# Weight sums in 64 DRAM transfers, gate weights ahead of the norm vectors, and a fixed plan for the norm between two projections

## The chip, the core and the metric

The kernel runs on one core of a Trainium2 chip. The metric is the device time of one execution in microseconds. The core has five engines, each with a queue of its own: TensorE (PE), VectorE (DVE), ScalarE (ACT), GpSimd (POOL) and SyncE (SP), which only issues transfers. DRAM and the on-chip buffers are joined by 16 DMA engines.

## What is computed

A small encoder with two mixer layers over 1024 tokens of width 1024, all in float32. Cut to what matters:

```python
for i in range(2):
    h = rms_norm(x, norm_g[i])
    y = mixer_a(h, ...) if i == 0 else mixer_b(h, ...)   # attention, 16 heads, ending in "@ w_out"
    x = x + y
    g = sigmoid(rms_norm(x, ple_norm_g[i]) @ ple_w_gate[i])
    x = x + g * (p[i] @ ple_w_proj[i])
return rms_norm(x, final_norm_g)
```

Between the output projection (`@ w_out`) and the gate projection (`@ ple_w_gate`) lies one RMS norm over the whole row of 1024, so a token tile can enter the gate projection only when both its halves have come out of the output projection.

## The kernel before

**Products.** A float32 product is made of three fast products: each operand is split into a high part (`wh`, `HTh`) and a low part (`wl`, `HTl`), and PE adds wh*HTh, wl*HTh and wh*HTl (L317). One [128 x 512] block with a contraction of 512 is 12 matmuls. Tokens are kept in 8 tiles of 128 rows. To enter a product, a normalised tile `xn` is transposed on PE four 128x128 pieces at a time (L445) into `t`, copied by ACT as `HTh` (L446), and DVE makes `HTl` (L447).

**Weights.** A queue object `WQ` brings weights in units of 512 KB. `stage` issues the load of a unit on SP (L209, into `wstage`), at most two units ahead of the split; `pump`, called once a step, splits one staged unit that is at least `age` steps old: ACT makes the high part (L226), DVE the low part one step later (L231). `hold` names a unit that isn't loaded yet.

**Mixer A (layer 0)** runs heads h = 0 to 15 with 8 steps j each. A step takes attention work of one head and fills PE with projection blocks. At j = 1 the bias table of the next head is built by POOL (L676, `tb<-MK,u`). POOL also multiplies the finished outputs by their gate (L531, `Y<-Y,G`) and by the softmax's reciprocal (L532, `Y<-Y,rb`), and SP stores them to DRAM (L524, `yD0h`). ACT's copy of a new output into a Y buffer (L497, `Y<-o`) has to wait for the store that last read that buffer.

**Weight sums.** The output projection is one Strassen level with sums of weight quarters, t1 to t4. `weight_sums` (L581 to L600) makes them in DRAM while mixer A runs, for both layers: 16 jobs of 1 MB, of which 8 are plain copies issued by SP (L589, as 16 rows of 16384) and 8 are accumulating transfers issued by POOL (L592, as 256 rows of 1024). A head from h = 1 on pops one job at j = 2 and one at j = 6 (L912).

**Dense phase.** `dense_phase(l)` (from L1437) follows each mixer. `strassen_out` yields after each of its last eight blocks, n = 0 to 7, in the order (5,0), (5,1), (3,0), (5,2), (3,1), (5,3), (3,2), (3,3); kind 5 completes a right half of tile 4+m, kind 3 that of tile m, each by one DVE addition (`fold`, L1388). Left halves are complete before: those of tiles 4 to 7 in the four "t4" blocks, those of tiles 0 to 3 by `second` (L1342). From n = 8 on the gate projection's first half (hf = 0) runs block by block in the order of tiles 0, 4, 0, 4, 1, 5, 1, 5 and so on. For the norm between them, ACT sums squares of half rows (L1473), DVE makes the reciprocal root of a pair of tiles m and 4+m (L1482 and ten small operations, L328 to L336), DVE scales the two tiles (L1500), and then the transposes follow. What is done at a step is decided by queues: `folded`, `squared`, `ready`, `pend`. At n = 0 two norm vectors are loaded (`load_gain`, L421), and then the gate weights are staged by `pump`; at n = 1 ACT takes the squares of all eight left halves in a row. A finished gate block is combined with `pp` (loaded from DRAM by L1593): L1541 (tanh), L1542, L1543. At the last tile of hf = 0 of layer 0, `rope_tables` has POOL make two tables (L1658) and SP store them with four transfers (L1661); after this the `pp` loads of hf = 1 are issued. In hf = 1 the finished tiles are squared, normed, and transposed for the next mixer (L1642, L445).

Of the kernel before, what the change touches and what calls it, by code (L numbers as in the profile page):

```python
# [11 lines left out]
F32 = mybir.dt.float32  # L12
# [9 lines left out]
NT = 8  # L22
# [136 lines left out]
def trunk(ctx, tc, x, wts, rpb, gains, hgains, mask, rope, gain0, out):  # L159
# [421 lines left out]
    def weight_sums():  # L581
        jobs = []

        def quarter(l, hf, u):
            i = UNIT["out", l, hf, u]
            return wts[i:i + 2]

        def copy(l, n, src):
            jobs.append(lambda: sync.dma_start(tD[l][n].rearrange("u p c -> (u p) c"), src.rearrange("u p c -> (u p) c")))  # L589

        def plus(l, n, src):
            jobs.append(lambda: pool.dma_start(tD[l][n].rearrange("u p c -> (u p) c"),  # L592
                                               src.rearrange("u p c -> (u p) c"), accum_op=ALU.add, max_dma_last_dim=4096))
# [666 lines left out]

    def strassen_out(l, X, ps_d, ps_t):
        xs = x if l == 0 else xD
# [174 lines left out]
    def dense_phase(l):  # L1437
        with ExitStack() as es:
# [20 lines left out]

            def pend_ht():  # L1460
                clock[0] += 1
                if pend and pend[0][0] <= clock[0]:
                    to_ht(ps_t, *pend.pop(0)[1:])

            ready = []
            folded, squared = [], []
            junk = one.tile([128, D], BF16, name="junk")
# [6 lines left out]

            def roots(n):
                if squared and squared[0][0] < n:
                    m = squared.pop(0)[1]
                    sm = slice(2 * m, 2 * m + 2)
                    r = sb.tile([128, 2], F32, name="rn", bufs=4)
                    wk = sb.tile([128, 8], F32, name="wkn", bufs=2)  # L1480
                    half = sa[:, 1, sm]
                    dve.scalar_tensor_tensor(half, half, 0.5 / D, sa[:, 0, sm], op0=ALU.mult, op1=ALU.add)  # L1482
                    rsqrt(r, half, wk)
                    ready.append(((m, 4 + m), r))

            def squares(n):
                while folded and folded[0][0] < n:
                    t = folded.pop(0)[1]
                    square(t, 1)
                    if t < 4:  # L1490
                        squared.append((n, t))

            def scale_pair():
                if not ready or len(pend) > 4:
                    return
                ts, r = ready.pop(0)
                xs = []
                for i, t in enumerate(ts):
                    xn = xalloc()
                    dve.scalar_tensor_tensor(xn, X[t], r[:, i:i + 1], g1, op0=ALU.mult, op1=ALU.mult)  # L1500
                    xs.append(xn)
                pend.extend([(clock[0] + 2, t, xn, (c,)) for c in range(2) for t, xn in zip(ts, xs)])

            for n, (step, m) in enumerate(strassen_out(l, X, ps_d, ps_t)):
                if n == 0:
# [3 lines left out]
                    WQ.cap[4] = 2  # L1509
                    WQ.hold = ("bg", 0) if l == 0 else None  # L1510
                    g1 = load_gain(sb, 2 * l + 1, 2)
                    g2 = load_gain(sb, 2 * l + 2, 2)
                    WQ.age, WQ.lag, age, lag = 2, 0, WQ.age, WQ.lag
                if n == 1:
                    for t in range(NT):
                        square(t, 0)
                if n == 2:
                    dve.tensor_scalar(sa[:, 0], sa[:, 0], 0.5 / D, 0.5 * EPS, op0=ALU.mult, op1=ALU.add)
                folded.append((n, m + 4 if step == 5 else m))
# [5 lines left out]
            WQ.age, WQ.lag = age, lag  # L1525

            for kind in ("ple",):
# [3 lines left out]
                for hf in range(2):  # L1531
# [69 lines left out]
                    for t, i in order:  # L1601
# [3 lines left out]
                        parts[t][i]()  # L1605
                        n += 1
                        WQ.pump()
                        pend_ht()
                        squares(n)
                        roots(n)  # L1610
                        scale_pair()
# [35 lines left out]
    def rope_tables(sb):  # L1647
# [3 lines left out]
        rt = sb.tile([128, 1024], F32, name="xn", bufs=4)  # L1651
        sync.dma_start(rt.rearrange("p (i t d) -> p i t d", i=2, t=NT), rope)
        for kind in range(2):
            ro = sb.tile([128, 1024], F32, name="xn", bufs=4)
            for i in range(2):
# [3 lines left out]
                                   rt[:, s].rearrange("p (t d) -> p t d", t=NT), gb, ALU.mult)  # L1659
            for i in range(2):  # L1660
                sync.dma_start(ropeD[kind, :, :, i].rearrange("t p d -> p t d"),  # L1661
                               ro[:, i * 512:(i + 1) * 512].rearrange("p (t d) -> p t d", t=NT))

# [24 lines left out]
```

## Time and profile before

| | |
|---|---|
| runs | 1551.56, 1554.64 and 1555.78 us, median 1554.64 us |
| profiled execution | 1561.72 us, of which its span is 1559.9 us |
| mean granted TensorE clock | 0.99 |
| busy time of PE | 1511.1 us (97%) in 8976 matmuls |
| busy time of DVE | 1097.7 us (70%) |
| busy time of ACT | 902.3 us (58%) |
| busy time of POOL | 287.1 us (18%) |
| transfers | 157.21 MB in 89943 packets, mean 101 GB/s |

The profiled execution is one of its own and 7.1 us slower than the median of the three runs. A row of the timeline gives start and duration of an instruction (or of several alike), its line, its operands as out<-in, and in brackets how long the engine was idle before it and what ended that. PEclk is the granted clock as a share of full speed. In these traces q1 is the queue of the transfers that SP issues, q0 that of POOL's.

Where things lie in time: mixer A up to about 545 us, the output projection of layer 0 up to about 622, its gate projection up to about 740, mixer B up to about 1370, then the dense phase of layer 1.

### The profile page before, as it was taken

How to read it: one execution, taken by the hardware profiler on the slowest of the kernel's cores; microseconds unless marked ns; L12 is line 12 of the kernel's file. 1: busy time of each engine (PE TensorE's matmuls, PEld its weight loads, DVE VectorE, ACT ScalarE, POOL GpSimd, SP SyncE). 2: the span in 40 equal slices, each digit the busy share in tenths (PEclk: the TensorE clock that was granted, in tenths of full speed). 3: DMA queues.
4: the chain of work that ended last, by engine and by line, in shares of the span. 5: the costliest groups of instructions: out<-in, count | busy, mean ns of one | idle time of the engine just before them, and what ended most of it. 6: DMA issues, size and time to landing. Idle time of an engine off the chain costs nothing.

```text
span 1559.9 us, 24298 instructions
## 1 busy us (share of the span) xinstructions
PE 1511.1 (97%) x8976; PEld 1319.8 (85%) x8976; DVE 1097.7 (70%) x2113; ACT 902.3 (58%) x1801; POOL 287.1 (18%) x389
## 2 busy tenths in 40 slices
PE   9998999999999999999999999999999999999897
PEld 8887988988988887778988889989999888778686
DVE  7564476477477598747877776777877777687856
ACT  6564465366366635433466767666767777644332
POOL 1311222113112000010132122453131200000022
PEclk9999999999999999999999999999999999999999
DMA  8325256242122862253210111111101112662214
GB/s 260 125 94 132 64 170 179 53 113 92 35 85 70 322 242 95 82 149 124 79 51 15 38 38 49 44 33 42 57 30 46 50 62 96 206 230 91 99 50 139
DMA packets 89943, 157.21 MB, mean 101 GB/s; under 512 B 17376, under 2 KB 53344, under 8 KB 89696
## 3 DMA queue, kind: packets, MB, share of 16 engines
q1 hardware_dynamic: 85056, 139.66, 26.8%
q0 software_dynamic: 2176, 8.39, 2.9%
q10 hardware_dynamic: 2592, 7.61, 1.4%
q8 instruction: 71, 1.16, 0.3%
q14 instruction: 48, 0.39, 0.1%
HBM read 125.10 MB, written 50.83 MB: 113 GB/s over the span
## 4 chain that ended last, share of the span: by engine, by line
PE 40%; DVE 7%; ACT 3%; issue 2%; DMA 0%; SPq 0%; ACTq 0%; DVEq 0%
PE d L317 19%; PE o L317 7%; PE t L1173 6%; PE s L317 6%; DVE PTl L1176 1%; DVE mn L1157 1%; ACT PTh L1175 1%; ACT P L1163 1%; PE t L317 1%; DVE wl L231 1%; PE t L445 0%; DMA wstage<-in_wts 0%; PE t L1127 0%; DVE t L991 0%; ACT wh L226 0%
## 5 line engine op out<-in xcount | busy, mean ns | idle before, releaser
L317 PE MATMUL d<-wh,HTh 128*128 128x256 f32 (+1 forms) x1032 | 348.9, 340 | 13.5 <-ACT th L642 7.7
L317 PE MATMUL d<-wh,HTl 128*128 128x256 f32 (+1 forms) x1032 | 342.1, 333 | 5.1 <-DVE HTl L447 5.1
L317 PE MATMUL d<-wl,HTh 128*128 128x256 f32 (+1 forms) x1032 | 341.1, 332 | 0.0
L1176 DVE TENSOR_TENSOR PTl<-t,PTh 128x512 fp32r<-128x512 f32 x256 | 164.4, 683 | 111.0 <-ACT PTh L1175 110.7
L317 PEld LDWEIGHTS d<-wh,HTh 128*128 128x128 f32 x1032 | 197.2, 192 | 35.2 <-ACT th L642 8.1
L317 PEld LDWEIGHTS d<-wh,HTl 128*128 128x128 f32 x1032 | 197.4, 192 | 25.7 <-DVE HTl L447 6.6
L317 PEld LDWEIGHTS d<-wl,HTh 128*128 128x128 f32 x1032 | 197.6, 192 | 19.1
L317 PE MATMUL d<-HTh,wh 128*128 128x512 f32 x504 | 205.8, 408 | 0.0
L317 PE MATMUL d<-HTh,wl 128*128 128x512 f32 x504 | 198.2, 393 | 0.0
L317 PE MATMUL d<-HTl,wh 128*128 128x512 f32 x504 | 197.5, 392 | 0.0
L1163 ACT ACTIVATE P<-s,mn 128x1024 f32<-128x1024 f32 x128 | 142.8, 1115 | 59.2 <-DVE mn L1157 58.4
L1175 ACT ACTIVATE PTh<-t 128x512 fp32r<-128x512 f32 x256 | 140.2, 593 | 44.6 <-PE t L1173 44.0
L1157 DVE TENSOR_REDUCE mn<-s 128x1 f32<-128x1024 f32 x128 | 154.7, 1209 | 12.2 <-PE s L317 12.2
L1173 PE MATMUL t<-ident,P 128*128 128x128 f32 x1024 | 137.2, 275 | 5.8 <-DVE PTl L1176 4.0
L317 PE MATMUL s<-KA,QS 128*128 128x512 f32 (+2 forms) x384 | 133.5, 402 | 0.0
L1173 PEld LDWEIGHTS t<-ident,P 128*128 128x128 f32 x1024 | 114.7, 140 | 21.0 <-DVE PTl L1176 15.3
L722 DVE TENSOR_TENSOR PTl<-t,PTh 128x384 fp32r<-128x384 f32 (+1 forms) x128 | 66.6, 520 | 85.2 <-ACT PTh L721 84.0
L231 DVE TENSOR_TENSOR wl<-wstage,wh 128x1024 fp32r<-128x1024 f32 x78 | 100.0, 1286 | 37.5 <-ACT wh L226 36.9
L317 PE MATMUL s<-KB,QS 128*128 128x512 f32 (+2 forms) x384 | 121.6, 371 | 0.0
L317 PE MATMUL o<-PTh,V 128*128 128x256 f32 (+2 forms) x672 | 118.9, 288 | 1.2 <-DVE Y L461 0.9
L317 PE MATMUL o<-PTl,V 128*128 128x256 f32 (+2 forms) x672 | 119.1, 288 | 0.1
L317 PEld LDWEIGHTS d<-HTh,wl 128*128 128x128 f32 x504 | 94.6, 188 | 21.7
(237 smaller groups left out, 2681.5 us busy)
## 6 DMA issues: line engine op xcount, KB each, us to landing
wstage<-in_wts SPq DMA_DIRECT2D x88, 512.0 KB
pp<-ppD SPq DMA_DIRECT2D x32, 256.0 KB
X<-in_x SPq DMA_DIRECT2D x15, 512.0 KB
rb<-rD SPq DMA_DIRECT2D x56, 128.0 KB
ppD<-th SPq DMA_DIRECT2D x20, 256.0 KB
xD<-X SPq DMA_DIRECT2D x8, 512.0 KB
X<-xD SPq DMA_DIRECT2D x8, 512.0 KB
out<-xn SPq DMA_DIRECT2D x7, 512.0 KB
```

The lines of the kernel that those rows point to most:

```text
L231: eng.tensor_tensor(lo[:, c:c + n], s[:, c:c + n], hi[:, c:c + n], ALU.subtract)
L317: pe.matmul(ps, a, b, start=first, stop=last, skip_group_check=True)
L722: dve.tensor_tensor(PTl[:, sl], ps[:, :m], PTh[:, sl], ALU.subtract)
L1157: dve.tensor_reduce(mn, ps, axis=AX.X, op=ALU.min)
L1163: act.activation(p, ps, AF.Exp, bias=mn, scale=-1.0, accum_out=RS[h, hf][:, t:t + 1])
L1173: pe.transpose(ps[:, i], p[:, k * 128:(k + 1) * 128], ident)
L1175: act.activation(PTh[:, ks, c], ps, AF.Copy)
L1176: dve.tensor_tensor(PTl[:, ks, c], ps, PTh[:, ks, c], ALU.subtract)
```

## The change

It has four parts.

1. Each copy and each accumulating transfer of the weight sums is cut in four: 64 jobs of 256 KB, copies of 16 rows of 4096 (L593 of the kernel after) and sums of 64 rows of 1024 (L597). One is popped at each step of a head but j = 1, from h = 1 on.
2. At the last `second`, before n = 0, the first two gate-weight units are staged at once, ahead of the loads of the norm vectors; `age` is 1 in place of 2 in these steps and 2 in the gate projection's first half. Units of the second half are held until n = 11.
3. The squares of the left halves are taken one by one, each right after the step that completes the half (`early`), and those of a right half right after its fold. The reciprocal roots, the scalings and the transposes follow a table (`norms`): roots and scaling of pair 0 at n = 3, of pair 1 at n = 5, the roots of pairs 2 and 3 together at n = 8, their scalings at n = 9 and n = 11. Transposes go up to two groups a step.
4. The four stores of the rope tables are issued after the `pp` load that follows tile 0 of hf = 1, in place of before the first `pp` loads of hf = 1.

```diff
         def copy(l, n, src):
-            jobs.append(lambda: sync.dma_start(tD[l][n].rearrange("u p c -> (u p) c"), src.rearrange("u p c -> (u p) c")))
+            for i in range(4):
+                jobs.append(lambda i=i: sync.dma_start(rows(tD[l][n], i, 4), rows(src, i, 4)))
 
         def plus(l, n, src):
-            jobs.append(lambda: pool.dma_start(tD[l][n].rearrange("u p c -> (u p) c"),
-                                               src.rearrange("u p c -> (u p) c"), accum_op=ALU.add, max_dma_last_dim=4096))
+            for i in range(4):
+                jobs.append(lambda i=i: pool.dma_start(rows(tD[l][n], i, 4), rows(src, i, 4),
+                                                       accum_op=ALU.add, max_dma_last_dim=4096))
...
-                        if h >= 1 and j in (2, 6) and jobs:
+                        if h >= 1 and j != 1 and jobs:
                             jobs.pop(0)()
...
             dve.tensor_tensor(xt, xt, P1[m], ALU.add)
+            early(1, m)
...
                 fold(xt0 + m, xc, Y[m], op)
+                if wk == "t4":
+                    early(4, m)
                 pulse()
...
-                pend.extend([(clock[0] + 2, t, xn, (c,)) for c in range(2) for t, xn in zip(ts, xs)])
+                    xs.append((t, xn))
+                pend.extend([(clock[0] + age + c, t, xn, (c,)) for c in range(2) for t, xn in xs])
...
+            norms = {
+                1: [prep],
+                3: [lambda: roots(0, 1), lambda: scale_pair(0)],
+                5: [lambda: roots(1, 1), lambda: scale_pair(1)],
+                8: [lambda: roots(2, 2)],
+                9: [lambda: scale_pair(2)],
+                11: [lambda: scale_pair(3)],
+            }
+
+            def early(kind, m):
+                if kind == 4:
+                    square(4 + m, 0)
+                if kind == 1 and m < 3:
+                    square(m, 0)
+                if kind == 1 and m == 3:
+                    square(3, 0)
+                    WQ.hold = ("ple", l, 1, 0)
+                    WQ.stage(True)
...
-                if n == 1:
-                    for t in range(NT):
-                        square(t, 0)
...
+                square(m + 4 if step == 5 else m, 1)
                 WQ.pump()
-                pend_ht()
-                squares(n)
-                roots(n)
-                scale_pair()
+                for f in norms.get(n, ()):
+                    f()
+                pend_ht(True)
...
                         if l == 0 and hf == 0 and t == seq[-1]:
-                            rope_tables(sb)
+                            rope_stores = rope_tables(sb)
                         load_pp(seq.index(t) + 2)
+                        if l == 0 and hf == 1 and t == 0:
+                            rope_stores()
```

**Mixer A, SP, around the store of the output that is copied at L497.** Before, the 1 MB copy stands ahead of `yD0h<-Y`:

```order
L524 DMA yD0l<-Y 128x4x128 [waits DMAHW3_49,DVE_49]
L670 DMA u<-U_90 128x384 [waits Pool_49]
L209 DMA wstage<-in_wts 128x1024 [waits DVE_49]
L589 DMA tD0t_83<-in_wts 16x16384
L524 DMA yD0h<-Y 128x4x128 [waits Pool_49]
L670 DMA u<-U_90 128x384 [waits DMAHW4_49,DMAHW0_49,Pool_49]
L209 DMA wstage<-in_wts 128x1024 [waits DMAHW1_49,DVE_49]
L468 DMA rD<-r8T 8x32 [waits DMAHW2_49,DVE_49]
```

In the kernel after:

```order
L675 DMA u<-U_90 128x384 [waits Pool_49]
L209 DMA wstage<-in_wts 128x1024 [waits DVE_49]
L593 DMA tD0t_83<-in_wts 16x4096 [waits DMAHW7_49]
L593 DMA tD0t_83<-in_wts 16x4096 [waits DMAHW0_49]
L524 DMA yD0h<-Y 128x4x128 [waits DMAHW1_49,Pool_49]
L593 DMA tD0t_83<-in_wts 16x4096 [waits DMAHW2_49]
L593 DMA tD0t_83<-in_wts 16x4096 [waits DMAHW3_49]
L675 DMA u<-U_90 128x384 [waits DMAHW5_49,DMAHW4_49,Pool_49]
```

Ahead of the store there are now two pieces of the copy, together half as large, and the other two are behind it.

**Mixer A, POOL, the accumulating transfers beside the table of a head.** Before:

```order
L676 TENSOR_TENSOR tb<-MK,u 128x128 x5
L592 DMA tD0t_80<-in_wts 256x1024
L592 DMA tD0t_82<-in_wts 256x1024
L676 TENSOR_TENSOR tb<-MK,u 128x128 x5
L531 TENSOR_TENSOR Y<-Y,G 128x512
L532 TENSOR_TENSOR Y<-Y,rb 128x512
L592 DMA tD0t_81<-tD0t_80 256x1024
```

In the kernel after:

```order
L681 TENSOR_TENSOR tb<-MK,u 128x128 x5
L597 DMA tD0t_80<-in_wts 64x1024 x4
L597 DMA tD0t_82<-in_wts 64x1024 x2
L681 TENSOR_TENSOR tb<-MK,u 128x128 x5
L531 TENSOR_TENSOR Y<-Y,G 128x512
L532 TENSOR_TENSOR Y<-Y,rb 128x512
L597 DMA tD0t_82<-in_wts 64x1024 x2
L597 DMA tD0t_81<-tD0t_80 64x1024
L531 TENSOR_TENSOR Y<-Y,G 128x512
```

Behind the table there are six pieces (1.5 MB) where there were two transfers (2 MB), and the rest comes in smaller groups behind later outputs.

**Dense phase of layer 0, SP, at the start of the norm.** The rows run from the last weights of the output projection over the norm vectors (`gain`) to the first `pp` loads. Before:

```order
L1278 DMA wstage<-in_wts 128x1024 x2
L421 DMA gain<-in_gains 128x1024 x2
L209 DMA wstage<-in_wts 128x1024 x6
L1593 DMA pp<-ppD_88 128x512 x4
L209 DMA wstage<-in_wts 128x1024 x2
```

In the kernel after:

```order
L1283 DMA wstage<-in_wts 128x1024 x2
L209 DMA wstage<-in_wts 128x1024 x2
L421 DMA gain<-in_gains 128x1024 x2
L209 DMA wstage<-in_wts 128x1024 x2
L1606 DMA pp<-ppD_88 128x512 x3
L209 DMA wstage<-in_wts 128x1024 x2
L1606 DMA pp<-ppD_88 128x512 x3
```

Two gate-weight loads have moved ahead of the two norm vectors.

**Dense phase of layer 0, SP, at the rope tables.** The rows run from the last gate weights of hf = 0 to the first store `xD` of a finished tile. Before:

```order
L209 DMA wstage<-in_wts 128x1024 x2
L1649 DMA th<-in_hgains 128x256
L1652 DMA xn<-in_rope 128x1024
L1661 DMA ropeD<-xn 128x8x64 x4
L1593 DMA pp<-ppD_88 128x512 x3
L1627 DMA xD<-X_5770 128x1024
```

In the kernel after:

```order
L209 DMA wstage<-in_wts 128x1024 x2
L1667 DMA th<-in_hgains 128x256
L1670 DMA xn<-in_rope 128x1024
L1606 DMA pp<-ppD_88 128x512 x3
L1684 DMA ropeD<-xn 128x8x64 x4
L1645 DMA xD<-X_5818 128x1024
```

The four stores of the tables have moved behind three `pp` loads; they still stand ahead of the first `xD` store.

More of the change, by code (lines that the diff above doesn't have):

```diff
@@ L1458, in salloc, with pend_ht @@
                 return stg.tile([128, D], F32, name="wstage")
-            def pend_ht():
+            def pend_ht(pairs=False):
                 clock[0] += 1
[L1462 to L1466, printed above, removed]
+                for _ in range(2 if pairs else 1):
+                    if pend and pend[0][0] <= clock[0]:
+                        to_ht(ps_t, *pend.pop(0)[1:])
             junk = one.tile([128, D], BF16, name="junk")
@@ L1473, in square @@
                 act.activation(junk[:, cs], X[t][:, cs], AF.Square, accum_out=sa[:, c, i:i + 1])
[L1475 to L1496, printed above, removed]
+            rn = {}
+            def roots(m, k):
+                sm = slice(2 * m, 2 * m + 2 * k)
+                r = sb.tile([128, 4], F32, name="rn", bufs=4)[:, :2 * k]
+                wk = sb.tile([128, 8], F32, name="wkn", bufs=2)
+                half = sa[:, 1, sm]
+                dve.scalar_tensor_tensor(half, half, 0.5 / D, sa[:, 0, sm], op0=ALU.mult, op1=ALU.add)
+                rsqrt(r, half, wk)
+                for i in range(k):
+                    rn[m + i] = r[:, 2 * i:2 * i + 2]
@@ L1505, in dense_phase @@
+            for n, (step, m) in enumerate(strassen_out(l, X, ps_d, ps_t, early)):
                 if n == 0:
@@ L1606, in dense_phase @@
                         n += 1
+                        if hf == 0 and n == 11:
+                            WQ.hold = ("bg", 0) if l == 0 else None
+                        if hf == 1:
+                            WQ.age, WQ.lag = age, lag
                         WQ.pump()
[L1608 to L1611, printed above, removed]
+                        for f in norms.get(n, ()):
+                            f()
+                        pend_ht(n < 20)
                         if i == 0:
```

32 lines of the change are left out of this document (18 added, 14 removed).

## Prediction

> **What bounds the kernel now.** I read the view of waits first, for PE alone. PE is busy for 97% of the span, so whatever can be won without removing a matmul lies in its pauses, and the view names who ends them.
>
> ```profile
> PE d L317 <- ACT th L642: 7.7, 2, 6.6
> PE d L317 <- DVE HTl L447: 5.1, 4, 2.0
> PE t L445 <- ACT junk L1473: 4.7, 2, 2.4
> ```
>
> The columns are total, times and longest. One pause of 6.6 us stands out, and the others are around 2 us in the step from output to gate projection. Next I read the granted clock in windows around the longest pauses, since a pause may cost more than itself.
>
> ```profile
> 144.00:150.00 6.00, 5.49 (x26) 5.50 (x27) 3.42 (x7) 2.57 (x6) 0.00 (x0) 0.51 0.00 1
> 617.00:625.00 8.00, 6.89 (x22) 5.29 (x23) 7.62 (x18) 2.31 (x5) 0.00 (x0) 0.57 0.18 68
> 640.00:646.00 6.00, 5.90 (x21) 4.76 (x22) 3.77 (x6) 2.50 (x7) 0.00 (x0) 0.72 0.59 211
> 700.00:710.00 10.00, 8.31 (x35) 6.76 (x36) 7.64 (x11) 4.72 (x8) 0.00 (x0) 0.83 0.57 201
> 802.00:808.00 6.00, 5.43 (x41) 5.09 (x42) 4.98 (x7) 3.90 (x8) 2.04 (x4) 1.00 0.28 98
> 1445.00:1455.00 10.00, 8.05 (x26) 6.36 (x27) 9.62 (x21) 3.94 (x10) 0.00 (x0) 0.66 0.20 67
> ```
>
> After the window come busy times of PE, PEld, DVE, ACT and POOL, then the clock. A window of length L at clock c loses (1 - c) x L: 2.9, 3.4, 1.7, 1.7 and 3.4 us, and nothing at 802. So a pause of 2 us costs up to 5.
>
> **Part 1, the weight sums.** The longest pause, traced back:
>
> ```profile
> 144.51 0.58 PE L317 MATMUL d<-wh,HTh 128*128 128x256 f32 x1 [6.62 <-ACT th L642]
> ...
> 143.24 0.59 ACT L497 ACTIVATE Y<-o 64x512 f32<-64x512 f32 x1 [9.90 <-DMA yD0h<-Y]
> ...
> 122.74 0.35 SPq L209 DMA_DIRECT2D wstage<-in_wts  x1
> 123.14 0.53 SPq L589 DMA_DIRECT2D tD0t<-in_wts  x1
> 123.70 0.58 SPq L524 DMA_DIRECT2D yD0h<-Y  x1
> ...
> 127.03 2.05 POOL L592 DMA_DIRECT2D tD0t<-in_wts  x2
> ...
> q0 software_dynamic: 544, 2.10, 41.7%
> ...
> 269.52 0.39 PE L317 MATMUL d<-wh,HTh 128*128 128x256 f32 x1 [1.06 <-ACT th L642]
> ```
>
> ACT stood at L497 for a Y buffer whose store had been issued 19 us before it landed. That store of 256 KB had 1.5 MB ahead of it on its own queue and met 2 MB of sums on POOL's queue (the q0 row is the stretch from 120 to 146 us), issued at 127.03. The same pattern four heads later gives the pause at 269.52. At stake are 6.62 + 2.9 + 1.06 = **10.6 us**. In the changed order half of the copy stands behind the store, so 1 MB is ahead of it, and the group of sums beside it is six pieces, 1.5 MB. The two ends for this edit are a gain of nothing (the store still meets the sums) and the whole 10.6. Two other stores tell which is nearer:
>
> ```profile
> 204.84 0.89 POOL L592 DMA_DIRECT2D tD0t<-tD0t  x1
> ...
> 204.93 0.37 SPq L524 DMA_DIRECT2D yD0h<-Y  x1
> ```
>
> This store was issued beside 1 MB of sums and nobody waited for it. By 143.24 - 123.70 = 19.5 us for what lay in the queues, half a MB less ahead should put the store some 2 us earlier, clear of the first sums. I take the whole 10.6. The 32 sums cost POOL issue time, about 0.9 us each by the row at 204.84 (32 x 0.9 = 29 us against 8 x 1.0), all of it in front of other POOL work in mixer A; POOL is busy for 18%, and its gate products wait for transfers anyway, so I count it at nothing; without that cover one table would come 6 x 0.9 = 5.4 us late, and PE with it.
>
> The Trainium skill, in "DMA: Bandwidth & Descriptors", section "Bandwidth", under "Measured", speaks against this part: batch DMAs to 1 MiB or more for at least 75% of peak; its section "Anatomy of one DMA" fits about 2.0 us plus bytes/436e3. By it one transfer of 1 MB takes an estimated 4.4 us and four of 256 KB take 10.4, so 64 pieces would lengthen the sums by an estimated 16 x 6 = 96 us in all. No run here shows a piece of 256 KB on POOL's queue; if the pieces hold the queue that long, it is the slower case below.
>
> **Parts 2 and 3, from output to gate projection.** First the state of DVE ahead of it:
>
> ```profile
> 560.00:600.00 40.00, 40.00 (x177) 32.85 (x175) 39.72 (x57) 15.53 (x22) 0.00 (x0) 1.00 0.34 123
> ```
>
> DVE is busy for 39.72 of 40 us, and PE runs 177 matmuls in 40, so a block of 12 takes 2.71. Then the step itself:
>
> ```profile
> 602.50 0.80 SPq L421 DMA_DIRECT2D gain<-in_gains  x2
> 603.34 17.51 SPq L209 DMA_DIRECT2D wstage<-in_wts  x5
> ...
> 609.56 1.06 ACT L226 ACTIVATE wh<-wstage 128x1024 fp32r<-128x1024 f32 x1 [2.38 <-DMA wstage<-in_wts]
> ...
> 606.68 0.68 DVE L1388 TENSOR_TENSOR X<-d,X 128x512 f32<-128x512 f32 x1
> ...
> 612.40 1.22 DVE L231 TENSOR_TENSOR wl<-wstage,wh 128x1024 fp32r<-128x1024 f32 x1
> 613.53 0.15 DVE L1482 SCALAR_TENSOR_TENSOR sa<-sa 128x2 f32<-128x2 f32 x1
> ...
> 615.69 2.48 DVE L1500 SCALAR_TENSOR_TENSOR xn<-X,rn,gain 128x1024 f32<-128x1024 f32 x2
> ...
> 600.76 0.47 PE L317 MATMUL d<-wh,HTh 128*128 128x512 f32 x1 [0.50 <-ACT junk L1473]
> ...
> 617.07 0.71 PE L445 MATMUL t<-ident,xn 128*128 128x128 f32 x4 [2.28 <-ACT junk L1473]
> ...
> 618.82 0.79 PE L317 MATMUL d<-wh,HTh 128*128 128x512 f32 x1 [1.04 <-DVE X L1388]
> ...
> 637.01 0.60 PE L445 MATMUL t<-ident,xn 128*128 128x128 f32 x4
> 637.36 0.48 PE L317 MATMUL d<-wh,HTh 128*128 128x512 f32 x1
> ...
> 640.10 0.50 PE L317 MATMUL d<-wh,HTl 128*128 128x512 f32 x1 [2.03 <-DVE HTl L447]
> ```
>
> The first gate weights are asked for at 603.34, behind the norm vectors, whose buffer came free only at 602.50. ACT splits the first at 609.56 and DVE makes its low part after that; only then come the root and the scaling (615.69), and the first tile is ready 1.2 us later, when PE has stood since 614.8. The view calls the releaser the squares, which ended long before; the operand is `xn`. The two pauses at 617.07 and 618.82, the one at 600.76 and the one at 640.10 with their dips are 2.28 + 1.04 + 0.50 + 2.03 + 3.4 + 1.7 = **10.95 us**. With the weights loaded ahead, ACT's idle 2.38 and DVE's wait behind it go, and eight squares in a row no longer stand ahead of ACT's splitting.
>
> What is late next is DVE. From the order after, from the fold at n = 1 to the low parts at n = 8, it has 7 folds and 8 low parts at 0.68 (10.2; each overlaps the next by some 0.08), 4 weight splits at 1.22 (4.9), 3 roots at 615.69 - 613.53 = 2.16 (6.5) and two scalings at 2.48 (5.0), in all 26.6, less the overlaps about 25.5. PE has seven blocks at 2.71 and eight groups of transposes at 637.36 - 637.01 = 0.35, together 21.8. So DVE exceeds PE by 3.7 us, and the ends are nothing (the transposes of n = 7 and n = 8 are first read four blocks later, which could absorb it) and 4.8 (no overlap). I take 3.7 of new waits, since 39.72 of 40 shows no slack carried in. They fall in several pieces at separate folds, each below the 1.4 us or so that left the clock at 1.00 in the 802 window, so no dip. That leaves 10.95 - 3.7 = **7.2 us**. The 11 operations saved by rooting two pairs at once are in that count.
>
> Layer 1 has the same step:
>
> ```profile
> 1445.83 0.63 PE L445 MATMUL t<-ident,xn 128*128 128x128 f32 x4 [2.42 <-ACT junk L1473]
> ...
> 1447.58 0.80 PE L317 MATMUL d<-wh,HTh 128*128 128x512 f32 x1 [1.12 <-DVE X L1388]
> ...
> 1469.18 0.50 PE L317 MATMUL d<-wh,HTl 128*128 128x512 f32 x1 [2.02 <-DVE HTl L447]
> ```
>
> 2.42 + 1.12 + 2.02 + 3.4 (the 1445 window) = 8.96, less 3.7, is **5.3 us**.
>
> On the dips the Trainium skill has a rule, in "TensorE: Matmul & The Clock Gate", section "HAM oscillation": no PE-idle gaps over about 3.4 us. By this rule only the pause of 6.62 would bring a dip, and the trace differs: the clock was 0.57 after 2.28 us. The sum goes by the windows; by the rule alone it would be 10.2 us smaller, an estimate that the windows contradict.
>
> **Part 4, the rope stores.**
>
> ```profile
> 685.38 4.12 SPq L1661 DMA_DIRECT2D ropeD<-xn  x4
> 689.54 4.69 SPq L1593 DMA_DIRECT2D pp<-ppD  x3
> ...
> 693.19 0.69 DVE L1542 SCALAR_TENSOR_TENSOR th<-th,pp 128x512 f32<-128x512 f32 x1 [8.99 <-DMA pp<-ppD]
> ...
> 701.69 0.63 PE L445 MATMUL t<-ident,xn 128*128 128x128 f32 x4 [3.17 <-DVE xn L1642]
> ```
>
> SP stood at the stores for POOL's tables from 685.38, so `pp` was asked for at 689.54 and DVE stood 8.99 us at 693.19; 8 us later the same delay reaches PE. Issued first, the `pp` loads go out about 4 us earlier and nothing of the stores' traffic is ahead of them. The stores then stand ahead of the first `xD` store, which nobody waits for soon. The ends are nothing and 3.17 + 1.7 = **4.9 us**; DVE's wait was almost three times PE's pause, so I take all of it.
>
> **Sum.** 10.6 + 7.2 + 5.3 + 4.9 = 28.0. The profiled execution took 1561.7 us, so 1533.7 by the profile; it was 7.1 us above the median of the runs, so **1527** beside that median.
>
> **Rivals.**
> - *DVE stays the bound in the step.* Its excess falls in one long wait a layer with a dip of 3.4 in place of small ones, and later low parts come late too: parts 2 and 3 then gain nothing of their 12.5, and 15.5 remain: 1539. For it speaks DVE at 39.72 of 40; against it, that the fixed plan puts the roots of two pairs behind the transposes.
> - *The store is still starved.* 1.5 MB of sums lie between the 1 MB that hurt nobody and the 2 MB that did, so the 10.6 stay: 28.0 - 10.6 = 17.4, which gives 1537.
> - *More stores are starved, slower than before.* Sums now follow at nearly every step. By the two rows of stores with a wait, more than 1 MB of sums in POOL's queue while a Y store is open is what decides; POOL's order after has such groups besides the first, at the end of layer 1's sums. If the pieces also hold the queue longer than their bytes need, the store at 204.93 and three like it between 201 and 327 us each cost what the first did, 6.62 + 2.9 = 9.5: four times that is 38, less the 17.4 of the other parts, so 21 slower: 1576. Against it: the stores stand ahead of the sums in time.
> - *The change doesn't do what it says.* The first gate weights still wait for a staging buffer, and new waits take what the old ones gave: 1553.
>
> **How the numbers follow.** Chances: the forecast 0.58 (its own range 1519, with no new waits, to 1533), DVE 0.11, the starved store 0.11, more starved stores 0.11, no effect 0.09. A measurement of this kernel can tell about 0.3%, 4.7 us, from no change. Faster by more is the first three, 0.80; within it 0.09; slower 0.11. The range starts at 1517, a little below the case in which all 35.4 us at stake are won (10.6 + 10.95 + 8.96 + 4.9, 1519), and reaches to 1551, over the two middle rivals, which leaves out the slower case and part of no effect.
>
> **What would show it.** Right: no ACT wait for `yD0h` at L497 and no pause of PE near 144 and 269; the first weight split of the gate projection no longer ended by a DMA; transposes without a pause of 2 us near 617 and 1445, with the clock at 1.00 in those windows; no wait of 9 us for `pp` at L1542. Wrong: a new wait for `yD0h` near one of the many sums, POOL's tables or gate products late for PE, folds waiting for DVE in pieces above 2 us with the clock low behind them.

## The result, and the profile after

The changed kernel takes 1530.57 us (median of 4 runs, 1529.42 to 1530.75) against 1553.3 us of the kernel before (median of 4, 1551.56 to 1555.78). The ratio is 0.9851, with a 95% interval of 0.9834 to 0.9868: 22.7 us faster by the medians. The profiled executions differ by more, 1561.72 and 1530.75 us, so 31.0.

The head of the page of the kernel after:

```profile
span 1529.0 us, 24364 instructions
PE 1499.0 (98%) x8976; PEld 1312.1 (86%) x8976; DVE 1099.1 (72%) x2091; ACT 899.6 (59%) x1801; POOL 305.0 (20%) x413
```

PE has the same 8976 matmuls in 12.1 us less busy time (1511.1 before): that is the clock (mean granted clock 0.999, before 0.990), not work. POOL is busy 17.9 us more, most of it for its smaller transfers: with part 1 alone (p1_sums below) it is 15.5 us more. The view of waits, for PE of the kernel after:

```profile
PE t L1178 <- DVE PTl L1181: 4.0, 3, 1.6
PE t L1132 <- DVE PTl L1181: 2.2, 5, 0.8
PE t L445 <- DVE HTl L447: 1.9, 3, 1.6
```

The rows that stood at the top before (7.7 for `th`, 4.7 for `junk`, 3.2 for `xn`) are gone; what is left first is a row of mixer B that was there before, and the third row, with its pause of 1.6 us, is new. The windows that answer to those of the prediction:

```profile
606.00:614.00 8.00, 7.85 (x44) 6.37 (x43) 6.78 (x10) 3.45 (x7) 0.00 (x0) 1.00 0.01 2
628.00:634.00 6.00, 6.00 (x32) 4.78 (x31) 6.00 (x9) 2.95 (x5) 0.00 (x0) 1.00 0.22 79
676.00:686.00 10.00, 10.00 (x51) 8.23 (x50) 7.56 (x10) 5.47 (x11) 0.00 (x0) 1.00 0.69 234
1424.00:1434.00 10.00, 9.82 (x51) 7.91 (x50) 8.41 (x19) 5.31 (x11) 0.00 (x0) 1.00 0.00 0
```

The clock is 1.00 in all of them. To see where the time went, I follow three matmuls that stand at the same places of the program: the first of the output projection of layer 0, the first of mixer B, the first of the output projection of layer 1. Timeline of the kernel before:

```profile
539.93 0.50 PE L317 MATMUL d<-wh,HTh 128*128 128x512 f32 x1 [0.74 <-ACT G L572]
...
740.60 0.39 PE L317 MATMUL d<-wh,HTh 128*128 128x256 f32 x1 [0.61 <-ACT th L1095]
...
1369.26 0.50 PE L317 MATMUL d<-wh,HTh 128*128 128x512 f32 x1 [0.74 <-ACT th L572]
```

and of the kernel after:

```profile
529.30 0.50 PE L317 MATMUL d<-wh,HTh 128*128 128x512 f32 x1 [0.74 <-ACT G L572]
...
716.09 0.39 PE L317 MATMUL d<-wh,HTh 128*128 128x256 f32 x1 [0.61 <-ACT th L1100]
...
1346.26 0.50 PE L317 MATMUL d<-wh,HTh 128*128 128x512 f32 x1 [0.74 <-ACT th L572]
```

By differences of these rows and the span's end, in the profiled executions:

| stage | before | after | difference | forecast |
|---|---|---|---|---|
| mixer A | 539.93 | 529.30 | -10.6 | -10.6 |
| dense phase, layer 0 | 200.67 | 186.79 | -13.9 | -12.1 |
| mixer B | 628.66 | 630.17 | +1.5 | 0 |
| dense phase, layer 1 | 190.64 | 182.74 | -7.9 | -5.3 |
| span | 1559.9 | 1529.0 | -30.9 | -28.0 |

Stage by stage the profile is near the forecast, with more won in both dense phases and a little lost in mixer B. The timed runs show 8 us less, and the experiments had to find where those are missing.

In the dense phase of layer 0 the gate weights are now asked for ahead of the norm vectors. Timeline of SP, kernel after:

```profile
586.54 2.02 SPq L209 DMA_DIRECT2D wstage<-in_wts  x2
591.88 0.80 SPq L421 DMA_DIRECT2D gain<-in_gains  x2
```

and on PE the transposes of the first tiles:

```profile
601.62 0.63 PE L445 MATMUL t<-ident,xn 128*128 128x128 f32 x4 [0.20 <-issue]
...
602.77 0.66 PE L445 MATMUL t<-ident,xn 128*128 128x128 f32 x4 [0.52 <-DVE xn L1498]
...
613.64 1.25 PE L445 MATMUL t<-ident,xn 128*128 128x128 f32 x8 [0.15 <-DVE HTl L447]
```

Where this step had pauses of 2.28, 1.04 and 2.03 us, it now has these of 0.20, 0.52 and 0.15. At the rope tables, SP of the kernel after:

```profile
659.73 7.58 SPq L1606 DMA_DIRECT2D pp<-ppD  x3
667.36 4.09 SPq L1684 DMA_DIRECT2D ropeD<-xn  x4
```

The `pp` loads of the second half no longer stand behind the stores, and DVE waits for no `pp` any more.

### The profile page after: what moved, and what is told of

Its sections match the earlier page's. It is cut to its first block, busy times and chain, and to the rows that moved or that the text cites. A ratio compares the mean times of both kernels' runs of the same rounds, so it can differ in the third digit from the quotient of the medians.

```text
span 1529.0 us, 24364 instructions
## 1 busy us (share of the span) xinstructions
PE 1499.0 (98%) x8976; PEld 1312.1 (86%) x8976; DVE 1099.1 (72%) x2091; ACT 899.6 (59%) x1801; POOL 305.0 (20%) x413
## 4 chain that ended last, share of the span: by engine, by line
PE 36%; DVE 10%; ACT 4%; issue 3%; DMA 0%; SPq 0%; ACTq 0%; DVEq 0%
PE d L317 17%; PE o L317 7%; PE t L1178 5%; PE s L317 5%; DVE PTl L1181 2%; DVE mn L1162 1%; ACT P L1168 1%; ACT PTh L1180 1%; PE t L317 1%; DVE xn L1498 1%; DVE QS L1142 0%; DVE wl L231 0%; DVE X L1394 0%; PE t L1132 0%; ACT wh L226 0%
## 5 line engine op out<-in xcount | busy, mean ns | idle before, releaser
L317 PE MATMUL d<-wh,HTh 128*128 128x256 f32 (+1 forms) x1032 | 343.0, 334 | 3.6 <-ACT HTh L446 0.8
L317 PE MATMUL d<-wh,HTl 128*128 128x256 f32 (+1 forms) x1032 | 337.9, 329 | 0.3 <-DVE HTl L447 0.3
L317 PE MATMUL d<-wl,HTh 128*128 128x256 f32 (+1 forms) x1032 | 337.2, 329 | 0.0
```

The lines of the kernel that those rows point to most:

```text
L317: pe.matmul(ps, a, b, start=first, stop=last, skip_group_check=True)
```

## The experiments

All kernels are judged beside runs of the kernel before on the same chip. "Medians" below means that of the changed kernel and that of the kernel before. A gain "by the ratio" is the distance of the ratio from 1, in microseconds of the median of before; the ratio comes out near that of the means, so single slow runs count in it, which the median leaves aside.

**Part 1 alone (p1_sums).** The kernel before with these lines:

```diff
-                        if h >= 1 and j in (2, 6) and jobs:
+                        if h >= 1 and j != 1 and jobs:
...
-            jobs.append(lambda: sync.dma_start(tD[l][n]..., src...))
+            for i in range(4):
+                jobs.append(lambda i=i: sync.dma_start(rows(tD[l][n], i, 4), rows(src, i, 4)))
```

and the same for the sums.

> The kernel before with part 1 alone (64 pieces, one at each step but j = 1). Theory A, the pause at 144 us is in every execution of the kernel before as large as in the profiled one: 10.6 us faster in the timed runs, 1553.3 - 10.6 = 1542.7, ratio 0.9932, with no wait of ACT for yD0h in the profile. Rival B, the profiled execution of before had a larger pause there than its timed runs, which were 8.4 us faster than it: the timed runs win only 2 to 3 us, near 1551, ratio 0.9985, though the profile shows the wait gone just the same. Rival C, pieces hold the queues: ACT waits for yD0h elsewhere, time 1553 or more.

Medians 1550.97 (12 runs, 1549.65 to 1552.37) and 1552.11 (28 runs, 1548.69 to 1561.53), ratio 0.9982 (0.9968 to 0.9996). No wait of ACT for `yD0h`; the first matmul of the output projection stands at 529.16 us, as in the kernel after. So the profile shows 10.8 us less and the timed runs 1.1 by the medians, 2.8 by the ratio: rival B, and theory A falls. What part 1 takes away is a tail: of the 28 runs of before 7 lay above 1555 us, of these 12 none above 1552.4; and the fastest run of before (1548.69) is no slower than the fastest here.

**Parts 2 and 3 alone (p23_step).** The kernel after with parts 1 and 4 undone:

```diff
-                        if h >= 1 and j != 1 and jobs:
+                        if h >= 1 and j in (2, 6) and jobs:
...
-                            rope_stores = rope_tables(sb)
+                            rope_tables(sb)
```

> The kernel before with parts 2 and 3 alone (gate weights ahead of the norm vectors, squares early, fixed plan). By the prediction 7.2 + 5.3 = 12.5 us, 1540.8, ratio 0.9920; by the profile of the kernel after, where the new waits came to 1.4 us in layer 0 in place of 3.7, up to 9.3 + 7.9 = 17 us, 1536, ratio 0.989. Rival, DVE remains the bound of the step: less than 4 us.

Medians 1538.79 (6 runs, 1535.5 to 1544.12) and 1552.11, ratio 0.991 (0.9889 to 0.9931): 13.3 to 14.0 us. In its profile the dense phases take 192.87 and 182.61 us, 7.8 and 8.0 less than before. DVE as the lasting bound falls.

**Part 4 alone (p4_rope).**

```diff
-                            rope_tables(sb)
+                            rope_stores = rope_tables(sb)
                         load_pp(seq.index(t) + 2)
+                        if l == 0 and hf == 1 and t == 0:
+                            rope_stores()
```

> The kernel before with part 4 alone (rope stores behind the first pp loads of the second half). By the prediction 4.9 us, 1548.4, ratio 0.9968, no wait of DVE for pp at L1542 and no pause of PE near 700. Rival: the later stores make the tables late for the next mixer, and 1 to 2 us of it are given back in mixer B: 1550.

Medians 1547.15 (11 runs) and 1552.11, ratio 0.9965 (0.9951 to 0.998): 5.0 to 5.4 us, by the prediction. The dense phase of layer 0 takes 195.36 us, 5.3 less; mixer B 628.94, so the later stores cost nothing there, and the rival falls.

The old sums are in this kernel and in p23_step, and their profiles hold the surprise. ACT in p4_rope:

```profile
139.15 0.59 ACT L497 ACTIVATE Y<-o 64x512 f32<-64x512 f32 x1 [5.17 <-DMA yD0h<-Y]
...
262.24 0.59 ACT L497 ACTIVATE Y<-o 64x512 f32<-64x512 f32 x1 [4.80 <-DMA yD0h<-Y]
```

ACT in p23_step:

```profile
134.69 0.59 ACT L497 ACTIVATE Y<-o 64x512 f32<-64x512 f32 x1 [1.45 <-DMA yD0h<-Y]
```

The same instruction, with the same transfers queued, waited 9.90 us in the profiled execution of before, 5.17 in p4_rope and 1.45 in p23_step. POOL issued its sums 3.33, 3.46 and 3.37 us behind the store in these three, so the times of issue don't tell them apart: the wait is the outcome of a race that changes from execution to execution. PE in p4_rope, behind the first of the two waits:

```profile
140.42 0.38 PE L317 MATMUL d<-wh,HTh 128*128 128x256 f32 x1 [1.90 <-ACT th L642]
```

In before PE stood 6.62 us behind 9.90, here 1.90 behind 5.17, and behind the 1.45 of p23_step it did not stand at all: about 3.27 us of a wait are absorbed before it reaches PE.

**Gate weights ahead, nothing else (p2_gate).** The kernel before with

```diff
             dve.tensor_tensor(xt, xt, P1[m], ALU.add)
+            if m == 3:
+                WQ.hold = ("bg", 0) if l == 0 else None
+                WQ.stage(True)
```

> The kernel before with only the first two gate-weight loads moved ahead of the norm vectors; squares, roots and transposes stay on their queues. If the late weights are what made the first tile late, the pauses at 617 and 1445 with their dips go, 2.28 + 1.04 + 3.4 and 2.42 + 1.12 + 3.4, up to 13.7 us: 1540. Rival: the eight squares in a row and the order of the roots are what made it late, then the split of the weights is early but the pauses stay, less than 3 us: 1551.

Medians 1547.59 (12 runs) and 1552.11, ratio 0.9974 (0.9958 to 0.9989). In layer 0 the pause of 2.28 us at the first transposes goes, but PE then stands later, at low parts that DVE makes late:

```profile
616.40 0.50 PE L317 MATMUL d<-wh,HTl 128*128 128x512 f32 x1 [2.08 <-DVE HTl L447]
...
629.81 0.50 PE L317 MATMUL d<-wh,HTl 128*128 128x512 f32 x1 [1.95 <-DVE HTl L447]
```

with the clock at 0.79 behind both (616 to 624 and 630 to 638 us). The dense phase of layer 0 takes 199.51 us, 1.2 less than before. The 4.5 us of the medians lie between what was expected and the rival: the early weights alone take one pause away and move the rest.

**The plan without the early weights (p3_plan).** The kernel before with parts 2 and 3, but

```diff
-                    WQ.hold = ("ple", l, 1, 0)
-                    WQ.stage(True)
+                    pass
```

and the hold set at n = 0.

> The kernel before with parts 2 and 3 but for the two gate-weight loads ahead of the norm vectors, which stay behind them. Parts 2 and 3 together gave 13.3 us by the medians, the two loads alone 4.5. If the parts add, the plan alone gives about 9, 1543. Rival: the plan needs the early weights, since its transposes and scalings are placed for them; alone it gives less than 5, above 1547, with a pause of PE behind the late weight split.

Medians 1547.12 (12 runs) and 1551.78 (29 runs), ratio 0.9964 (0.9948 to 0.998): 4.7 to 5.6 us, near the rival. One timeline of its SP shows why, with the weights behind the norm vectors again:

```profile
592.68 0.80 SPq L421 DMA_DIRECT2D gain<-in_gains  x2
593.53 10.61 SPq L209 DMA_DIRECT2D wstage<-in_wts  x4
```

and on PE the two groups of transposes now wait together:

```profile
607.25 2.26 PE L445 MATMUL t<-ident,xn 128*128 128x128 f32 x8 [5.00 <-issue]
```

The operand `xn` was scaled from 605.86 on, behind a weight split that DVE had waited 6.15 us for. Alone the two halves give 4.5 and 4.7 us, together 13.3: a plan that places DVE's work needs the weights to be there, and early weights need the plan.

**The last copy behind the store (a_first).** The kernel before, all transfers of 1 MB:

```diff
-                            jobs.pop(0)()
+                            if h in (2, 6) and j == 6:
+                                HELD.append(jobs.pop(0))
+                            else:
+                                jobs.pop(0)()
...
-                post.add(YS[layer] + 2, lambda: store(0, Y))
+                post.add(YS[layer] + 2, lambda: (store(0, Y), [HELD.pop(0)() for _ in range(len(HELD))]))
```

> The kernel before, all weight sums of 1 MB and at their places, but the last copy of each layer is issued right behind the store yD0h<-Y in place of right ahead of it. Theory S, the store has to start before POOL's sums do, and what stands ahead of it on its own queue decides: no wait of ACT for yD0h in the profile, 1 to 3 us faster in the timed runs, near 1550, with their spread as small as the 2.7 us of the run with part 1 alone. Rival X, only the amount of sums in flight beside the store counts: waits of 1 to 10 us stay, the time is that of before and the spread over 5 us.

Medians 1551.57 (12 runs, 1549.82 to 1553.26) and 1551.78 (29 runs, 1549.47 to 1559.59), ratio 0.9991 (0.9978 to 1.0004). No wait for `yD0h` at either place, and a spread of 3.4 us against 10.1 (none of the 12 runs above 1555 us, 7 of the 29). Theory S holds for the wait and the spread; the gain of 1 to 3 us that it expected is not shown, since the interval includes 1.

**Twice the copy ahead of the store (a_2copy).**

```diff
+                        if h in (2, 6) and j == 6:
+                            sync.dma_start(spare[0]..., wts[0:2]...)
                         if h >= 1 and j in (2, 6) and jobs:
```

> The kernel before with a further copy of 1 MB on SP ahead of the last copy at heads 2 and 6 (into memory that nobody reads), so 2.5 MB ahead of the store. Theory S: the store always comes behind the sums' start, ACT waits for yD0h at both places in the profile, by 10 us or more, and the timed runs are 10 to 20 us slower, 1562 to 1572. Rival X: the copy adds no wait for yD0h, the time is within 3 us of before.

Medians 1570.42 (4 runs) and 1551.78, ratio 1.012 (1.0087 to 1.0154). ACT:

```profile
145.13 0.59 ACT L497 ACTIVATE Y<-o 64x512 f32<-64x512 f32 x1 [11.42 <-DMA yD0h<-Y]
...
270.04 0.59 ACT L497 ACTIVATE Y<-o 64x512 f32<-64x512 f32 x1 [4.26 <-DMA yD0h<-Y]
```

The store loses the race at both places, as it did in the profiled execution of before, and PE stands 8.15 and 0.99 us behind the two waits; the second wait is shorter than the 10 us expected. This profile is of the fastest of the four runs (1564.33 us); all four are slower than any of the 29 of before. Rival X falls: with a_first, more or less ahead of the store on its own queue makes the runs slower or takes the wait away.

**Twice the sums beside it (a_2sum).**

```diff
+                        if h in (3, 7) and j == 6:
+                            for i in range(2):
+                                pool.dma_start(spare[i]..., wts[2 * i:2 * i + 2]...)
```

> The kernel before with two further transfers of 1 MB on POOL's queue behind the pair of sums at heads 3 and 7 (into memory that nobody reads), so 4 MB beside the store. Theory S: the store still meets the sums in some executions and then waits longer than the 9.9 us seen, up to twice; the timed runs are 0 to 10 us slower and spread more than before. Rival X: every execution waits some 20 us at both places, 20 us or more slower, 1573 and above.

Medians 1554.26 (10 runs, 1550.92 to 1562.66) and 1551.78, ratio 1.0013 (0.9995 to 1.0032); in its profile no wait at the first place and 3.15 us at the second. Doubling the sums does not make every execution wait: X falls here too. The longer waits that theory S allowed for did not show either, and the slower median is not clear of the noise. It fits a store that is through before the sums start and so doesn't care how many follow, but that is argued: the trace shows when a store landed only where ACT waited for it.

**All but part 1 (p234).** The kernel after with the weight sums as before:

```diff
-                        if h >= 1 and j != 1 and jobs:
+                        if h >= 1 and j in (2, 6) and jobs:
```

> The kernel after with part 1 undone (the sums and copies of 1 MB at j = 2 and 6 as before). If part 1 is worth in the timed runs what it gave alone, 1 to 3 us, this is near 1532.5 with a spread of 5 us or more, since the store meets the sums in some executions. Rival, part 1 is worth the 10.6 us of the profiled execution: 1541.

Medians 1534.47 (5 runs, 1530.15 to 1534.67) and 1556.15 (11 runs), ratio 0.9856 (0.9828 to 0.9883). Its profile has the wait at the second place:

```profile
260.97 0.59 ACT L497 ACTIVATE Y<-o 64x512 f32<-64x512 f32 x1 [6.49 <-DMA yD0h<-Y]
...
262.24 0.58 PE L317 MATMUL d<-wh,HTh 128*128 128x256 f32 x1 [3.21 <-ACT th L642]
```

Part 1 is worth up to 3.9 us beside the kernel after by the medians, which were not taken beside each other, and less than 1 by the ratios. The two kernels that follow, b_first and b_pool, were timed beside p234 on one chip and have no wait for `yD0h`; they are 4.4 and 3.6 us faster than it by the medians. None of this is the 10.6 of one execution.

**The kernel after with 1 MB sums and the copy behind the store (b_first).** p234 and the edit of a_first.

```diff
+                            if h in (2, 6) and j == 6:
+                                HELD.append(jobs.pop(0))
```

> The kernel after with part 1 replaced by sums and copies of 1 MB as before, but the last copy of each layer issued behind the store yD0h<-Y. If the place of the copy is all that part 1 does to the time, this equals the kernel after, 1530.6 within 1 us, and its spread is as small (1.3 us). Rival: the smaller pieces help by themselves, then it is 1 to 2 us slower than the kernel after.

Medians 1530.09 (6 runs, 1528.7 to 1531.21) and 1556.15, ratio 0.9838 (0.9812 to 0.9864); no wait for `yD0h`, the output projection starts at 529.00 us. It equals the kernel after within the 1 us expected, and b_pool, which has the 64 pieces, within 0.8 us on the same chip: the order of one copy and one store does what the 64 pieces do. Its spread of 2.5 us is not as small as the 1.3 expected.

**POOL's last products later (b_pool).**

```diff
-                                pool.tensor_tensor(X[t][:, cs], X[t][:, cs], gt[:, cs], ALU.mult)
+                                late.append(lambda t=t, cs=cs: pool.tensor_tensor(...))
+                            for _ in range(2):
+                                if late and n >= 17:
+                                    late.pop(0)()
```

> The kernel after with POOL's eight products of the last layer's left halves with the gain (L1640) put off to the end of the first half of the gate projection. In the kernel after two of them run beside DVE's scaling of pair 3, whose two instructions take 3.53 us there in place of 2.48, and beside one L1555 of 1.42 in place of 0.69; the pause of 1.55 us before the transposes at 1447 follows. If POOL's work is what lengthens DVE's, the scaling takes 2.48 again, that pause falls below 0.5 us, and the time is 1 to 1.5 us lower, 1529.3. Rival: DVE's instructions are longer for another reason, then durations and pause stay, 1530.6.

1530.87 (5 runs), ratio 0.9843 (0.9816 to 0.9869). It did not test what it was to test: the products ran at 1440.55 and 1444.02 us all the same. POOL has nothing else to do there, and a place further back in the program holds an engine back only behind its own instructions.

**The same products on DVE (b_dve).**

```diff
-                                pool.tensor_tensor(X[t][:, cs], X[t][:, cs], gt[:, cs], ALU.mult)
+                                late.append(lambda t=t, cs=cs: dve.tensor_tensor(...))
...
+                        if late and n >= 16:
+                            late.pop(0)()
```

> The kernel after with the eight products of the last layer's left halves with the gain (L1640) done by DVE, one a step from n = 16 on, in place of POOL as soon as a half is finished. This really keeps POOL idle beside the scaling of pair 3, which the run b_pool did not: there POOL's products stood at the same times (1440.55 and 1444.02), since an engine's queue holds back only its own instructions. If POOL's work is what lengthens DVE's, the two scalings take 2.48 us in place of 3.52, L1555 takes 0.69 in place of 1.41, and the pause of 1.5 us at 1447 falls below 0.5; the time is about 1.5 us lower than the kernel after, 1529, at the edge of what five rounds tell. Rival: the durations stay, and 1530.6.

1527.94 (5 runs, 1527.1 to 1529.09) beside 1552.5, ratio 0.9838 (0.982 to 0.9856). DVE in the kernel after, with POOL's products at 1440.41 and 1443.88:

```profile
1440.85 1.42 DVE L1555 SCALAR_TENSOR_TENSOR th<-th,pp 128x512 f32<-128x512 f32 x1 [1.27 <-ACT th L1554]
...
1442.91 3.53 DVE L1498 SCALAR_TENSOR_TENSOR xn<-X,rn,gain 128x1024 f32<-128x1024 f32 x2
```

and here:

```profile
1440.51 0.69 DVE L1556 SCALAR_TENSOR_TENSOR th<-th,pp 128x512 f32<-128x512 f32 x1 [1.28 <-ACT th L1555]
...
1441.85 2.47 DVE L1498 SCALAR_TENSOR_TENSOR xn<-X,rn,gain 128x1024 f32<-128x1024 f32 x2
```

The durations are 0.69 and 2.47 again, and the pause of 1.55 us before the transposes at 1447 is gone. All five runs lie below all four of the kernel after, but they were not taken beside each other, and the intervals of the two ratios overlap; b_first, which leaves POOL's products in place, has the same ratio of 0.9838. So the durations and the pause are shown, and that the time falls by 2.6 us is not settled.

## Why the prediction was right, and which term was not

**Part 1: the mechanism right, its size not that of a timed run.** The prediction put 10.6 us on the wait for `yD0h`, and the profiled executions differ by just that. But the step that sized it took one execution for all. The profiled execution of before was one in which the store lost its race badly. These are all profiled executions with the mixer A of the kernel before; the start of the output projection is the end of that stage:

| run | ACT's wait, first place | PE's pause | ACT's wait, second place | PE's pause | mixer A ends |
|---|---|---|---|---|---|
| before | 9.90 | 6.62 | 4.33 | 1.06 | 539.93 |
| p4_rope | 5.17 | 1.90 | 4.80 | 1.52 | 533.93 |
| p234 | 0 | 0 | 6.49 | 3.21 | 533.83 |
| p2_gate | 0 | 0 | 4.58 | 1.30 | 530.82 |
| p3_plan | 1.79 | 0 | 0 | 0 | 530.12 |
| p23_step | 1.45 | 0 | 0 | 0 | 529.24 |

Each has a wait at one place at least. The six profiled executions with the pieces, or with the copy behind the store, have none, and there mixer A ends between 529.00 and 530.12 us. PE's pause is each time about 3.27 us shorter than ACT's wait (in a_2copy too), and a wait shorter than that does not reach PE. So the price of the wait runs from nothing to 10.6 us, and the prediction took the highest of the six for all. In the timed runs part 1 alone is worth 1.1 us by the medians, 2.8 by the ratio. The prediction had the hint in hand: that execution was 7.1 us above the median of the runs, and the last step of the sum took those 7.1 as an offset that both kernels share. They were most of the very pause that the change removes: without it the profiled execution of p1_sums took 1550.60 us. The kernel after has no such offset (1530.75 in the profile, 1530.57 in the median).

The reason for the race was argued from SP's order and holds: one copy less ahead of the store and no wait (a_first, b_first, the pieces), one more ahead and a long wait (a_2copy). The store wasn't issued earlier, though; SP of the kernel after:

```profile
122.88 1.13 SPq L593 DMA_DIRECT2D tD0t<-in_wts  x2
124.10 0.53 SPq L524 DMA_DIRECT2D yD0h<-Y  x1
124.67 1.15 SPq L593 DMA_DIRECT2D tD0t<-in_wts  x2
```

124.10 us against 123.70 before. What it has ahead in its queue is what changed. That the transfer itself then started earlier, as the prediction had it, the trace doesn't show.

POOL's longer issue was hidden, as forecast: mixer A ends at 529.30 us with 32 sums and at 529.00 with 8 (b_first).

The Trainium skill asks for transfers of 1 MiB or more for at least 75% of peak ("DMA: Bandwidth & Descriptors", section "Bandwidth", under "Measured"). The trace of the kernel after agrees with it in part. A 256 KB sum landed in 4.1, 6.7 and 10.1 us (least, median, most):

```profile
DMA to landing us min/median/max: 4.1/6.7/10.1
```

where one of 1 MB took 8.4, 11.9 and 15.7 before. A quarter of the bytes takes more than half the time to land, so a piece is dearer for its size; but the packets of POOL's queue took only 3.1% of the 16 engines' span against 2.9%. Added up by the medians, the landings of the sums come to 214 us against 95, but they overlap with each other and with the work, and mixer A ends no later for it. POOL itself now stands 7.0 us in all for earlier pieces of its own sums (L597), which it did not before.

**Parts 2 and 3: right, and the new waits were over-sized.** 12.5 us were forecast, 13.3 to 14.0 came in the timed runs. The ledger charged DVE's excess of 3.7 us a layer as new waits. They came to 0.50 + 0.20 + 0.52 + 0.15 = 1.4 in layer 0 and 0.18 + 1.55 = 1.7 in layer 1. DVE in the kernel after shows where the rest went:

```profile
602.63 1.28 DVE L1394 TENSOR_TENSOR X<-d,X 128x512 f32<-128x512 f32 x2
```

Two folds run back to back after the scaling; PE had gone on past the first of them without a pause, since the kernel has four PSUM buffers for these results. The excess was a delay of DVE, not of PE. No pause of more than 2 us was left, and no clock below 1.00 in the windows above, as forecast. The forecast put the pauses at 617 and 1445 us down to the late weights and the squares ahead of their splitting, and did not say that one half of the cure is worth little without the other. Either half alone leaves the clock low (0.79 behind the pauses of p2_gate, 0.50 from 607 to 613 us in p3_plan, behind one pause of 5.00 us), and only both together remove it.

**Part 4: right.** 4.9 forecast, 5.0 by the medians and 5.4 by the ratio of p4_rope, and the wait for `pp` is gone.

**The sum.** By the medians of the parts alone 1.1 + 13.3 + 5.0 = 19.4 us, by their ratios 2.8 + 14.0 + 5.4 = 22.2; measured 22.7 by the medians. The forecast of 28.0 is too large by 5.3 us. Part 1 alone falls 7.8 to 9.5 us short of its term; the other parts gave 0.9 to 2.0 more than theirs, and all together gave 0.5 to 3.3 more than the parts added up, which fits part 1 being worth more beside the others (3.6 and 4.4 us, b_pool and b_first against p234) than alone. So that 1527 came within 3.6 us of the measured time is in part luck: the range would have held the result with part 1 at nothing. Mixer B, 1.5 us longer in the profile after, was forecast unchanged. It takes 628.53 us in p1_sums, 629.58 in p23_step, 629.53 in p2_gate, 629.97 in a_first, so 1.3 of the 1.5 us are there in a_first too, which has none of parts 2 to 4; what makes it so stays open.

The rivals: the starved store was half right in an unforeseen way, since the old kernel itself is starved to a degree that changes between executions, in two of the six above by less than reaches PE. More starved stores did not happen: no kernel with the pieces shows a wait for `yD0h`. DVE did not stay the bound (p23_step), and the change is not without effect.

## What to carry to other kernels

A long wait in one profiled execution is one draw: before its price enters a sum, ask why that execution is slower than the timed runs, and look for the same instruction in other profiles of the same code, and for how much of the wait is absorbed before it reaches the engine that bounds the kernel. A store that a computing engine will wait for belongs ahead of bulk copies in its queue; changing that order did here what cutting every transfer in four did. And where an engine is full for a stretch, early operands and a plan for its work have to come together: each alone gave a third.

## What was not expected of the hardware

- Two instructions of DVE took 3.53 us in place of 2.47, and one 1.42 in place of 0.69, while POOL ran a product of its own on other data; with POOL idle they were short again (b_dve).
- The race between POOL's queue and SP's: with identical queues, one wait came out between 0 and 9.90 us in six profiled executions, and 14 of 57 timed runs of the kernel before lay above 1555 us, where none of 24 did beside them with the copy cut or moved (p1_sums, a_first).
- A pause of about 2 us lowers the clock only at times: in the kernel before 0.72 behind 2.03 us at 640.10 and 1.00 behind 2.02 us at 1469.18, in p2_gate 0.72 behind 1.95 us at 629.81, in p4_rope 1.00 behind 1.90 us at 140.42; no pause of 1.6 us or less in the kernel after did.
